# RWKV-7 stage of a fused three-block kernel: group norm a round later, hops over 0.86 of the round, 256-column scores, attention's first operands loaded in the last round

## The chip, the cores and the metric

The kernel runs on one core of a Trainium2 chip. The metric is the device time of one execution in microseconds, the median of several runs. The change is compared by the same median.

## The reference, cut to what matters

Three blocks follow one another on a residual stream of 1024 tokens by 1024 features, in float32: a mixing block (stick-breaking attention, HGRN and GLA), a block of RWKV-7 time mix plus dilated window attention, and a block of spatial gating plus Fourier mixing. The change touches the second one. Its RWKV part, for 16 heads of 64:

```python
xs = tuple(t.astype(jnp.float32).transpose(1, 0, 2, 3)
           for t in (r_h, w_h, k_h, v_h, -kk, kk * a_h))
def step(state, inp):
    r_t, w_t, k_t, v_t, av_t, bv_t = inp
    sa = jnp.einsum('bhvk,bhk->bhv', state, av_t)
    state = (state * w_t[:, :, None, :] + sa[..., None] * bv_t[:, :, None, :]
             + v_t[..., None] * k_t[:, :, None, :])
    return state, jnp.einsum('bhvk,bhk->bhv', state, r_t)
...
y = ((y - mu) * lax.rsqrt(var + GN_EPS)).reshape(B, S, RWKV_W) * ln_x_w + ln_x_b
bonus = jnp.sum(r_h * k_h * r_k, axis=-1, keepdims=True) * v_h
return (y + bonus.reshape(B, S, RWKV_W)) * jax.nn.silu(gate)
```

The scan is computed in chunks of 64 tokens. The window attention then works on q and k of the same block, in three dilations.

## The kernel before, in words

Every large projection is a float32 product made of three fp32r matmuls (operands split into a high and a low part; lines L310 to L312, called dense below). Weights come in on the SP queue (L280), ScalarE casts the high part (L281) and VectorE subtracts the low part (L282).

The RWKV stage (898 to 1932 us of the span) handles 16 units, each a pair of heads by half of the tokens (8 chunks of 64). It runs in 18 rounds `it`. In a round a planner, `interleave`, merges several generators: the one that is least far along its own stretch of the round goes next. A generator is given as (generator, number of steps n, a, b): its step k is due at a + (b - a) k / n of the round. `PLAN` holds a and b: [0] the chain, [1] the inverse, [2] the features, [3] the dense work. The compiled program fixes the order on every engine from this, engine by engine.

- `rw_feat`, unit `it`: decays, keys, bonus; then the scores, M1 and A, from 128x128 matmuls on tiles M and "At" (`BK`) into PSUM "mx" (L1116), masked by VectorE (L1118).
- `rw_inverse`, unit `it - 1`: a triangular inverse. A goes to DRAM (L1141) and back as "At" (L1143), 31 row steps run on VectorE (L1161 and L1163), the result goes by DRAM to XS (L1167, L1170), then small matmuls finish it (L1182, L1188). The features' `BK` and the inverse's At are one buffer.
- `rw_chain`, unit `it - 2`: the recurrence over 8 chunks in three hops each. h1 (L1219) reads the state SV, its result is copied to R by VectorE (L1220) and ScalarE (L1221). h2 (L1225) makes the corrected values in PSUM "ch", copied to SV by VectorE (L1226) and ScalarE (L1227). h3 (L1230) gives the next state (L1234 on VectorE, with sd of L1223), and L1235 the output. Behind the eighth chunk come two ScalarE evictions and the group norm: sums (L1242, L1248), a square root (L753 on VectorE, L754 on POOL), the scaling (L1250), four transposes into "ch" (L1257), four ScalarE evictions (L1261), and the bonus and the gate (L1263, L1264).
- `rw_dense` and `att_jobs`: projections; `ATT[it]` is how many attention projections a round takes.

Behind the 18 rounds the attention opens its pools, and `at_load` of its first unit U[0] fetches q and k (L1407, "qkr"), casts them (L1411, L1421) and subtracts (L1413, L1422); then the scores run (L1447).

Of the kernel before, what the change touches and what calls it, by code (L numbers as in the profile page):

```python
# [13 lines left out]
ALU = mybir.AluOpType  # L14
# [159 lines left out]
ATT = [1, 2] * 3 + [1, 0, 1, 1, 0, 1, 1, 1, 3, 2, 2, 2]  # L174
# [8 lines left out]
GNY = 8  # L183
# [6 lines left out]
QS = 1  # L190
RORD = [("gate", [128, 512], 2), ("tt", [128, 512], 2), ("sd", [128, 64], 2), ("R", [128, 64], 2), ("gst", [128, 24], 2),
        ("ast", [128, 512], 1), ("vst", [128, 256], 1), ("dc", [128, 8], 3), ("bv", [128, 512], 1), ("bw", [128, 512], 1),
# [8 lines left out]
PLAN = [(0.0, 1.0), (0.0, 0.5), (0.05, 0.8), (0.0, 1.0)]  # L201


class Kern:
# [774 lines left out]
    def rwkv(self):  # L979
        nc, tc, I = self.nc, self.tc, self.I  # L980
        with tc.tile_pool(name="rw", bufs=1, reuse_waits="tile") as rw, self.psum(mx=2, iv=1, ch=1, cy=1):
# [14 lines left out]
            att = iter(self.att_jobs())  # L996
            for it in range(18):
# [11 lines left out]
        self.rk_pool.__exit__(None, None, None)  # L1009
# [18 lines left out]
    def rw_feat(self, rw, S):
        nc, I = self.nc, self.I
        V, TT = nc.vector, nc.vector.tensor_tensor  # L1030
        ff = lambda n: self.t(rw, [128, 512], n, bufs=1)
# [7 lines left out]
        wa = self.t(rw, [128, 128], "wa", bufs=1)  # L1039
# [10 lines left out]
        e1 = self.t(rw, [128, 8, 65], "E1")  # L1050
# [18 lines left out]
        n2 = self.t(rw, [128, 8], "n2", bufs=2)  # L1069
# [18 lines left out]
        S["bv"] = self.t(self.dp, [128, 512], "bvd", bufs=3)  # L1088
        bv = self.t(rw, [128, 512], "bv", bufs=1)
# [5 lines left out]
        BK = self.t(rw, [128, 8, 128], "At", bufs=1)  # L1095
# [14 lines left out]
        for c0 in (0, 4):  # L1110
# [710 lines left out]
```

## Time and profile before

| what | value |
|---|---|
| median of 3 runs | 2780.82 us (2775.7 to 2782.38) |
| the profiled execution's own time | 2780.22 us |
| its span | 2778.4 us, mean granted clock 0.99 |
| TensorE busy over the span | 2693.8 us (97%) |
| VectorE | 1743.9 us (63%) |
| ScalarE | 1168.3 us (42%) |
| POOL | 262.0 us (9%) |
| DMA | 274.49 MB, mean 99 GB/s |

PE is TensorE's matmuls, PEld its weight loads, which overlap the matmuls; DVE is VectorE, ACT ScalarE, SP the engine whose queue issues most DMAs. A wait is put on the instruction that stood and on the one that released it. A busy share says little of a stage: the rows below are taken from the stages that the change touches.

### The profile page before, as it was taken

How to read it: one execution, taken by the hardware profiler on the slowest of the kernel's cores; microseconds unless marked ns; L12 is line 12 of the kernel's file. 1: busy time of each engine (PE TensorE's matmuls, PEld its weight loads, DVE VectorE, ACT ScalarE, POOL GpSimd, SP SyncE). 2: the span in 40 equal slices, each digit the busy share in tenths (PEclk: the TensorE clock that was granted, in tenths of full speed). 3: DMA queues.
4: the chain of work that ended last, by engine and by line, in shares of the span. 5: the costliest groups of instructions: out<-in, count | busy, mean ns of one | idle time of the engine just before them, and what ended most of it. 6: DMA issues, size and time to landing. Idle time of an engine off the chain costs nothing.

```text
span 2778.4 us, 49283 instructions
## 1 busy us (share of the span) xinstructions
PE 2693.8 (97%) x18584; PEld 2245.1 (81%) x18584; DVE 1743.9 (63%) x4636; ACT 1168.3 (42%) x2829; POOL 262.0 (9%) x366
## 2 busy tenths in 40 slices
PE   8999999999998999999999999999999999999999
PEld 7878787878776787778877777888889989978887
DVE  4675643443966568786788877673476776644344
ACT  4443323233323335444455455444565665432232
POOL 0000000000202000100111011000111211100100
PEclk9999999999999999999999999999999999999999
DMA  3111121115751322222222222223664553432132
GB/s 127 54 61 50 50 67 42 58 63 177 243 198 64 93 82 66 74 76 79 63 72 69 71 72 76 88 81 102 198 179 147 160 167 103 132 115 61 50 122 98
DMA packets 214142, 274.49 MB, mean 99 GB/s; under 512 B 70000, under 2 KB 105616, under 8 KB 213776
## 3 DMA queue, kind: packets, MB, share of 16 engines
q1 hardware_dynamic: 185904, 218.90, 26.4%
q10 hardware_dynamic: 28000, 52.44, 5.2%
q8 instruction: 146, 2.39, 0.4%
q14 instruction: 92, 0.75, 0.1%
HBM read 211.49 MB, written 59.77 MB: 98 GB/s over the span
## 4 chain that ended last, share of the span: by engine, by line
PE 42%; DVE 6%; issue 3%; ACT 3%; DMA 3%; POOL 1%; ACTq 0%; SPq 0%; DVEq 0%; POOLq 0%
PE pd L310 8%; PE pd L312 8%; PE pd L311 8%; PE po L1525 2%; PE mx L310 2%; PE mx L311 2%; PE mx L312 2%; PE mx L1116 1%; PE tr L1535 1%; PE sc L1447 1%; PE cy L1219 1%; PE sc L1448 1%; DVE wl L282 1%; DMA qkr<-qkg 1%; PE ch L1230 1%
## 5 line engine op out<-in xcount | busy, mean ns | idle before, releaser
L310 PE MATMUL pd<-aH,wh 128*128 128x512 f32 x1808 | 752.9, 417 | 11.9 <-ACT aH L305 7.9
L312 PE MATMUL pd<-aH,wl 128*128 128x512 f32 x1808 | 725.6, 401 | 2.2 <-DVE wl L282 2.2
L311 PE MATMUL pd<-aL,wh 128*128 128x512 f32 x1808 | 725.1, 401 | 1.4 <-DVE aL L306 1.4
L282 DVE TENSOR_TENSOR wl<-wraw,wh 128x512 fp32r<-128x512 f32 (+1 forms) x412 | 295.1, 722 | 287.1 <-ACT wh L281 282.7
L281 ACT CAST wh<-wraw 128x512 fp32r<-128x512 f32 (+1 forms) x412 | 249.8, 612 | 416.3 <-PE pd L311 221.9
L310 PEld LDWEIGHTS pd<-aH,wh 128*128 128x128 f32 x1808 | 344.8, 191 | 74.5 <-ACT aH L305 8.1
L312 PEld LDWEIGHTS pd<-aH,wl 128*128 128x128 f32 x1808 | 344.0, 190 | 72.8 <-DVE wl L282 3.6
L311 PEld LDWEIGHTS pd<-aL,wh 128*128 128x128 f32 x1808 | 345.1, 191 | 58.0 <-DVE aL L306 2.3
L310 PE MATMUL pd<-wh,aH 128*128 128x256 f32 (+1 forms) x976 | 288.1, 297 | 4.5 <-ACT wh L281 2.7
L311 PE MATMUL pd<-wl,aH 128*128 128x256 f32 (+1 forms) x976 | 279.2, 287 | 2.6 <-DVE wl L282 2.6
L312 PE MATMUL pd<-wh,aL 128*128 128x256 f32 (+1 forms) x976 | 277.1, 286 | 0.3 <-DVE aL L306 0.3
L310 PEld LDWEIGHTS pd<-wh,aH 128*128 128x128 f32 x976 | 186.0, 191 | 8.5 <-ACT wh L281 3.5
L311 PEld LDWEIGHTS pd<-wl,aH 128*128 128x128 f32 x976 | 186.5, 191 | 6.5 <-DVE wl L282 4.1
L312 PEld LDWEIGHTS pd<-wh,aL 128*128 128x128 f32 x976 | 186.1, 191 | 1.9 <-DVE aL L306 0.7
L1223 ACT ACTIVATE sd<-SV,dc 64x64 f32<-64x64 f32 x256 | 88.4, 345 | 106.3 <-DVE SV L1234 96.4
L1500 ACT ACTIVATE S<-S,anm 128x256 f32<-128x256 f32 (+1 forms) x256 | 118.1, 464 | 16.1 <-DVE anm L1493 16.1
L1161 DVE TENSOR_TENSOR Xt<-At,X 128x60 f32<-128x60 f32 (+24 forms) x496 | 105.1, 212 | 10.5 <-DMA At<-dA 1.0
L1163 DVE TENSOR_TENSOR X<-X,Xt 128x60 f32<-128x60 f32 (+24 forms) x496 | 105.2, 212 | 10.3
L1451 DVE CUSTOM_DVE_ANT_0 S<-sc,cf 128x256 f32<-128x256 f32 (+1 forms) x256 | 85.8, 377 | 38.9 <-PE sc L1448 25.7
L1219 PEld LDWEIGHTS cy<-SV,M 128*128 128x128 f32 x512 | 81.4, 189 | 23.8 <-DVE SV L1234 11.7
L1447 PE MATMUL sc<-kk,qq 128*128 128x256 f32 (+1 forms) x256 | 91.3, 371 | 7.8 <-DVE kk L1422 6.9
L1448 PE MATMUL sc<-kk,ql 128*128 128x256 f32 (+1 forms) x256 | 86.8, 350 | 0.0
(385 smaller groups left out, 4653.6 us busy)
## 6 DMA issues: line engine op xcount, KB each, us to landing
wraw<-in_w2fm SPq DMA_DIRECT2D x122, 256.0 KB, 2.8
wraw<-in_w1fm SPq DMA_DIRECT2D x80, 256.0 KB, 2.6
qkr<-qkg SPq DMA_DIRECT2D x152, 128.0 KB, 2.9
wraw<-in_w2out SPq DMA_DIRECT2D x64, 256.0 KB, 3.3
sgd<-s ACTq DMA_DIRECT2D x48, 256.0 KB, 2.2
sgt<-sgd SPq DMA_DIRECT2D x48, 256.0 KB, 3.5
qkg<-ast ACTq DMA_DIRECT2D x40, 256.0 KB, 2.1
wraw<-in_w3fm SPq DMA_DIRECT2D x38, 256.0 KB, 2.6
```

The source lines that it names most:

```text
L281: nc.scalar.copy(h, raw)
L282: nc.vector.tensor_tensor(l, raw, h.bitcast(F32), ALU.subtract)
L310: mm(ps, lh, rh, start=start, stop=False)
L311: mm(ps, lh, rl, start=False, stop=False)
L312: mm(ps, ll, rh, start=False, stop=stop)
L1161: eng.tensor_tensor(tmp[:, :M, :n], At[:, j:j + 1, j + 1:32].to_broadcast([128, M, n]), X[:, :M, j:j + 1].to_broadcast([128, M, n]), ALU.mult)
L1163: eng.tensor_tensor(X[:, :M, j + 1:32], X[:, :M, j + 1:32], tmp[:, :M, :n], ALU.add)
L1219: nc.tensor.matmul(xy[:, c, n], M1[:, c, n], sv[:, c, n], start=c % 4 == 0 and n == 0, stop=False, skip_group_check=True)
L1223: nc.scalar.activation(sd[s], sv[s, c, n], AF.Identity, scale=dc[s])
L1447: mm(o, q, k, start=i == 0, stop=False, skip_group_check=True)
L1448: mm(o, ql, k, start=False, stop=i == len(args) - 1, skip_group_check=True)
L1500: nc.scalar.activation(x, x, AF.Exp, bias=nm[:, n, h, t:t + 1], accum_out=l[:, n, h, t:t + 1])
```

## The change

The group norm leaves the end of `rw_chain` and becomes a generator of its own, `rw_fin`, for unit `it - 3`, so a round later; the last one runs alone after the rounds. The hops' plan goes from 38 steps in (0, 1.0), of which 24 are hops, to 24 steps in (0, 0.86). The scores take two head halves in one 256-column matmul, per pair of chunks; the masks follow. The inverse is planned over (0, 0.9) in place of (0, 0.5), with six steps between the X loads and their use, the features over (0.03, 0.92). `at_load` of U[0] moves into round 17, and its eight loads from the ACT queue to SP. The gate is computed in even rounds. `rf` is a new pool for the features and the inverse that is closed ahead of round 17. The attention projections are spread so that each round holds about 48 dense steps.

```diff
-ATT = [1, 2] * 3 + [1, 0, 1, 1, 0, 1, 1, 1, 3, 2, 2, 2]
+ATT = [1, 2] + [0, 2] * 6 + [2, 2, 2, 3]
...
-GNY = 8
...
-QS = 1
...
-PLAN = [(0.0, 1.0), (0.0, 0.5), (0.05, 0.8), (0.0, 1.0)]
+PLAN = [(0.0, 0.86), (0.0, 0.9), (0.03, 0.92), (0.0, 1.0)]
...
             for it in range(18):
                 gens = []
+                if it == 17:
+
+                    rf_pool.__exit__(None, None, None)
+                    self.rk_pool.__exit__(None, None, None)
+                    self.aqk_pool = tc.tile_pool(name="aqk", bufs=1, side="right", reuse_waits="tile")
+                    self.aqk = self.aqk_pool.__enter__()
+                    self.AU = [dict(p=u % 8, hf=u // 8) for u in range(16)]
+                    gens.append((self.at_load(self.aqk, self.AU[0]), 4, 0.2, 0.9))
                 if it >= 2:
-                    gens.append((self.rw_chain(rw, U[it - 2]), 30 + GNY, *PLAN[0]))
+                    gens.append((self.rw_chain(rw, U[it - 2]), 24, *PLAN[0]))
+                if it >= 3:
+                    gens.append((self.rw_fin(rw, U[it - 3]), 6, 0.1, 0.75))
                 if 1 <= it <= 16:
-                    gens.append((self.rw_inverse(rw, U[it - 1]), 37, *PLAN[1]))
+                    gens.append((self.rw_inverse(rw, rf, U[it - 1]), 42, *PLAN[1]))
                 if it < 16:
-                    gens.append((self.rw_feat(rw, U[it]), 22, *PLAN[2]))
+                    gens.append((self.rw_feat(rw, rf, U[it]), 23, *PLAN[2]))
                 jobs = list(islice(att, ATT[it]))
-                gens.append((chain(*jobs, self.rw_dense(rw, it)), 32 * (it < 14) + 16 * (it == 15) + 16 * len(jobs), *PLAN[3]))
+                n = 32 * (it < 14 and it % 2 == 0) + 16 * (it % 2 == 1 and it < 14) + 16 * (it % 2 == 0 and it >= 2)
+                gens.append((chain(*jobs, self.rw_dense(rw, it)), n + 16 * len(jobs), *PLAN[3]))
                 interleave(gens)
+            for _ in self.rw_fin(rw, U[15]):
+                pass
             self.late_jobs = list(att)
...
-        if odd and p < 8:
+        if not odd and p:
             g = [self.t(rw, [128, 512], "gate", bufs=2) for _ in range(2)]
-            self.gate[p] = g
-            yield from self.dense_gen(self.I["w2fm"][25 + p], self.tanh_gate_ev(rw, g, ("ast", 1)), self.acts)
-
-    def rw_feat(self, rw, S):
+            self.gate[p - 1] = g
+            yield from self.dense_gen(self.I["w2fm"][24 + p], self.tanh_gate_ev(rw, g, ("ast", 1)), self.acts)
...
         rm = self.c("rmask")
-        for c0 in (0, 4):
-            cs = slice(c0, c0 + 4)
+        for c0 in range(0, 8, 2):
+            cs = slice(c0, c0 + 2)
+            pv = self.mm_ps().rearrange("p (c n t) -> p c n t", c=2, n=2)
+            for c in range(2):
+                nc.tensor.matmul(pv[:, c].rearrange("p n t -> p (n t)"), BK[:, c0 + c], M1[:, c0 + c].rearrange("p n t -> p (n t)"),
+                                 start=True, stop=True)
             for n, (s, x, mk) in enumerate(((E, O, rm[:, 0:128]), (O, E, rm[:, 64:192]))):
-                ps = self.mm_ps()
-                pv = ps.rearrange("p (c t) -> p c t", c=4)
-                for c in range(4):
-                    nc.tensor.matmul(pv[:, c], BK[:, c0 + c], M1[:, c0 + c, n], start=True, stop=True)
                 for d, h in ((A, s), (M1[:, :, n], x)):
-                    TT(d[h, cs], pv[h], mk[h].unsqueeze(1).to_broadcast([64, 4, 128]), ALU.mult)
-                yield
+                    TT(d[h, cs], pv[h, :, n], mk[h].unsqueeze(1).to_broadcast([64, 2, 128]), ALU.mult)
+            yield
...
             nc.sync.dma_start(xs[o:o + 32, :, 64 * (g // 2) + b:64 * (g // 2) + b + 32], dX[g].rearrange("c r i -> r c i"))
-        yield
-
-        Y1 = self.t(rw, [128, 8, 32], "Xt", bufs=1)
...
             nc.tensor.matmul(xy[:, c].rearrange("p n v -> p (n v)"), A[:, c], both, start=False, stop=c % 4 == 3, skip_group_check=True)
             yield
-
-        y, sq, st = ff(), ff(), self.t(rw, [128, 24], "gst", bufs=2)
-        bc = lambda a: a.unsqueeze(2).to_broadcast([128, 8, 64])
+        S["y"] = y = self.t(rw, [128, 512], "tt", bufs=2)
         nc.scalar.copy(c8(y)[E], xy[E, :, 1])
         nc.scalar.copy(c8(y)[O], xy[O, :, 0])
+
+    def rw_fin(self, rw, S):
+
+        nc = self.nc
+        V, TT = nc.vector, nc.vector.tensor_tensor
+        p, hf, y = S["p"], S["hf"], S["y"]
+        E, O = slice(0, 64), slice(64, 128)
+        c8 = lambda a: a.rearrange("p (c t) -> p c t", c=8)
+        ff = lambda: self.t(rw, [128, 512], "tt", bufs=2)
+        gate = self.gate[p][hf]
+        bw = self.t(rw, [128, 512], "bw", bufs=1)
+        nc.sync.dma_start(bw, S["bv"])
+        sq, st = ff(), self.t(rw, [128, 24], "gst", bufs=2)
+        bc = lambda a: a.unsqueeze(2).to_broadcast([128, 8, 64])
         V.tensor_reduce(st[:, 0:8], c8(y), AX.X, ALU.add)
         V.tensor_scalar(st[:, 0:8], st[:, 0:8], -1.0 / 64, None, ALU.mult)
         TT(c8(y), c8(y), bc(st[:, 0:8]), ALU.add)
         nc.scalar.activation(sq, y, AF.Square)
         yield
-        yield
         V.tensor_reduce(st[:, 8:16], c8(sq), AX.X, ALU.add)
         self.rsqrt(rw, st[:, 16:24], st[:, 8:16], 1.0 / 64, 64e-5)
+        yield
+        yield
         TT(c8(y), c8(y), bc(st[:, 16:24]), ALU.mult)
-        for _ in range(GNY):
-            yield
+        yield
         z = ff()
         zv = z.rearrange("p (c two t) -> p c two t", two=2, t=64)
         yt = self.mm_ps("ch")
...
-                for _ in self.at_load(aqk, U[0]):
-                    pass
                 self.consts(at, "c3")
...
-                    (nc.scalar if p + hf == 0 and QS else nc.sync).dma_start(x[s], self.qkg[row][src, cols])
+                    nc.sync.dma_start(x[s], self.qkg[row][src, cols])
```

On TensorE, in the middle of a unit's hops before the change: h1 (L1219), the dense matmuls behind it, h2 (L1225) and h3 (L1230). `R` and `SV` are what the copies write.

```order
L1219 MATMUL cy_11414<-SV_1536_8924,M_1790_10421 128x64
L311 MATMUL pd_11561<-aL_1099_7105,wh_11452 128x512
L312 MATMUL pd_11561<-aH_1098_7104,wl_11453 128x512
L310 MATMUL pd_11561<-aH_1098_7104,wh_11452 128x512
L311 MATMUL pd_11561<-aL_1099_7105,wh_11452 128x512
L1225 MATMUL ch_11595<-R_11598,XS_1534_8922 128x64
L312 MATMUL pd_11561<-aH_1098_7104,wl_11453 128x512
L1068 MATMUL mx_11625<-cf_157,fs_11624 128x2 x4
L310 MATMUL pd_11561<-aH_1098_7104,wh_11452 128x512
L311 MATMUL pd_11561<-aL_1099_7105,wh_11452 128x512
L312 MATMUL pd_11561<-aH_1098_7104,wl_11453 128x512
L1230 MATMUL ch_11596<-SV_1536_8924,M_1816_10627 128x128
```

The changed program has new line numbers: dense is L308 to L310, h1 L1227, h2 L1233, h3 L1238, the transposes L1277. The same place in a unit's hops, on TensorE, in the changed program:

```order
L308 MATMUL pd_12201<-aH_1098_7104,wh_12084 128x512
L1227 MATMUL cy_11870<-SV_1536_8924,M_1881_10942 128x64
L1277 MATMUL ch_12217<-cf_157,tt_11846 128x128 x4
L1227 MATMUL cy_11870<-SV_1536_8924,M_1881_10942 128x64
L309 MATMUL pd_12201<-aL_1099_7105,wh_12084 128x512
L310 MATMUL pd_12201<-aH_1098_7104,wl_12085 128x512
L308 MATMUL pd_12201<-aH_1098_7104,wh_12084 128x512
...
L308 MATMUL pd_12201<-aH_1098_7104,wh_12090 128x512
L309 MATMUL pd_12201<-aL_1099_7105,wh_12090 128x512
L1233 MATMUL ch_12228<-R_12231,XS_1534_8922 128x64
```

The transposes, which stood behind the last hop, now stand between the two halves of an h1, and the next h2 takes the next tile of "ch". Between h1 and h2 there were four dense matmuls, now ten (five of them in the gap marked by dots).

On VectorE before the change, around the masks (L1118) of a unit; L1243 is of the norm, L1179 of the inverse:

```order
L947 SCALAR_TENSOR_TENSOR rkv_2564_14942<-last_14943,pf,rkv_2564_14942 128x1
L1243 TENSOR_SCALAR gst_15180<-gst_15180 128x8
L948 SCALAR_TENSOR_TENSOR rkv_2564_14942<-pd_15109,pf,rkv_2564_14942 128x511
L1118 TENSOR_TENSOR A_14991<-mx_15120,cf_8920 64x512
L1118 TENSOR_TENSOR M_2577_14989<-mx_15120,cf_8920 64x4x128
L1118 TENSOR_TENSOR A_14991<-mx_15140,cf_8920 64x512
L1118 TENSOR_TENSOR M_2577_14989<-mx_15140,cf_8920 64x4x128
L1118 TENSOR_TENSOR A_14991<-mx_15156,cf_8920 64x512
L1118 TENSOR_TENSOR M_2577_14989<-mx_15156,cf_8920 64x4x128
L1179 STREAM_TRANSPOSE Xt_15045<-XS_1534_8922 32x256
L1118 TENSOR_TENSOR A_14991<-mx_15171,cf_8920 64x512
L1118 TENSOR_TENSOR M_2577_14989<-mx_15171,cf_8920 64x4x128
```

On VectorE in the changed program, around the masks (L1129) of a unit; L1234 is the SV copy of a hop, L1242 the new state, L1228 the R copy:

```order
L1129 TENSOR_TENSOR A_15447<-mx_15534,cf_8919 64x256
L1129 TENSOR_TENSOR M_2661_15445<-mx_15534,cf_8919 64x2x128
L1129 TENSOR_TENSOR A_15447<-mx_15534,cf_8919 64x256
L1129 TENSOR_TENSOR M_2661_15445<-mx_15534,cf_8919 64x2x128
...
L1129 TENSOR_TENSOR M_2661_15445<-mx_15567,cf_8919 64x2x128
L1234 COPY SV_1535_8923<-ch_15551 64x64
L1129 TENSOR_TENSOR A_15447<-mx_15602,cf_8919 64x256
...
L1129 TENSOR_TENSOR M_2661_15445<-mx_15602,cf_8919 64x2x128
L1242 SCALAR_TENSOR_TENSOR SV_1535_8923<-ch_15552,dc_13916,sd_15553 64x64 x2
L1129 TENSOR_TENSOR A_15447<-mx_15624,cf_8919 64x256
...
L1129 TENSOR_TENSOR M_2661_15445<-mx_15624,cf_8919 64x2x128
L1228 COPY R_15640<-cy_15134 64x64
```

Where the masks were a block, hops' copies now stand among them, and each mask is half as wide.

On SP before the change, from the end of the RWKV stage into the attention; L227 is a constant, L1346 the residual r, L1407 are operands of attention:

```order
L280 DMA wraw_20201<-in_w2fm 128x512
L227 DMA cf_20069<-in_c 128x784
L1346 DMA r_3425_20030<-hd 128x1024
...
L1346 DMA r_3428_20033<-hd 128x1024
L1435 DMA ag_20155<-qkg 128x512
L1437 DMA vn_20156<-vd 128x4x128
L1346 DMA r_3421_20026<-hd 128x1024
L1346 DMA r_3422_20027<-hd 128x1024
L1407 DMA qkr_20071<-qkg 64x512 x2
L1407 DMA qkr_20111<-qkg 64x512 x2
```

On SP in the changed program, from the last weight loads of round 17 (L278) on; L1425 are the operands of U[0], L225 the constant, L1363 r:

```order
L278 DMA wraw_19756<-in_w2v 128x512
L1425 DMA qkr_19544<-qkg 64x512 x2
L1425 DMA qkr_19625<-qkg 64x512 x2
L1425 DMA qkr_19703<-qkg 64x512 x2
L1425 DMA qkr_19821<-qkg 64x512
L278 DMA wraw_19762<-in_w2v 128x512
L1425 DMA qkr_19821<-qkg 64x512
...
L278 DMA wraw_20348<-in_w2fm 128x512
L225 DMA cf_20072<-in_c 128x784
L1363 DMA r_3434_20062<-hd 128x1024
```

The loads of U[0] were on the ACT queue, and now stand on SP among weight loads, ahead of the constant and of r.

## Rows read from the trace of the kernel before

**Rows 1.** Windows, RWKV stage: length, busy (instructions) of PE, PEld, DVE, ACT, POOL, PEclk, DMA share, GB/s
```profile
898.00:1932.00 1034.00, 1007.56 (x6573) 822.28 (x6574) 756.61 (x2287) 476.16 (x1176) 96.39 (x151) 1.00 0.26 75
```
**Rows 2.** Waits of weight loads in the RWKV stage: us in total, times, longest
```profile
PEld ch L1230 <- ACT SV L1227: 25.4, 65, 1.1
PEld ch L1225 <- ACT R L1221: 24.3, 57, 1.5
PEld ch L1257 <- DVE tt L1250: 12.7, 7, 2.5
PEld cy L1219 <- DVE SV L1234: 11.7, 26, 1.1
```
**Rows 3.** Timeline at one h2 (start, us, engine line, [idle before and releaser])
```profile
1099.71 0.40 PE L312 MATMUL pd<-aH,wl 128*128 128x512 f32 x1
...
1099.94 0.40 PE L310 MATMUL pd<-aH,wh 128*128 128x512 f32 x1
...
1101.42 0.30 PEld L1225 LDWEIGHTS ch<-R,XS 128*128 128x128 f32 x2 [1.52 <-ACT R L1221]
```
**Rows 4.** Timeline at the transposes of one norm
```profile
1397.94 1.09 DVE L1250 TENSOR_TENSOR tt<-tt,gst 128x512 f32<-128x512 f32 x1 [1.83 <-POOL gst L754]
...
1399.09 0.66 PE L1257 MATMUL ch<-cf,tt 128*128 128x128 f32 x4 [1.94 <-DVE tt L1250]
```
**Rows 5.** Windows behind two long waits (columns as in rows 1)
```profile
1400.10:1403.50 3.40, 3.40 (x10) 2.62 (x9) 2.54 (x5) 3.27 (x8) 0.00 (x0) 0.50 0.00 0
1946.20:1953.00 6.80, 3.74 (x13) 3.35 (x14) 2.37 (x7) 1.83 (x3) 0.00 (x0) 0.50 0.87 275
```
**Rows 6.** Waits of weight loads from 1932 to 1965 us
```profile
PEld sc L1447 <- DVE kk L1422: 7.7, 2, 6.8
```
**Rows 7.** Timeline of the attention's start, SP, ACT and PE
```profile
1934.22 10.52 SPq L1346 DMA_DIRECT2D r<-hd  x4
...
1938.67 2.55 ACTq L1407 DMA_DIRECT2D qkr<-qkg  x4
...
1946.84 0.62 ACT L1411 CAST qq<-qkr 128x512 fp32r<-128x512 f32 x1 [4.97 <-DMA qkr<-qkg]
...
1949.26 0.48 PE L1447 MATMUL sc<-kk,qq 128*128 128x128 f32 x1 [6.41 <-DVE kk L1422]
```
**Rows 8.** Timeline, score matmuls (L1116), and 257-column ones (L1694), with the next dense
```profile
948.46 1.06 PE L1116 MATMUL mx<-M,At 128*128 128x128 f32 x8
949.27 0.47 PE L310 MATMUL pd<-aH,wh 128*128 128x512 f32 x1
...
2530.85 3.62 PE L1694 MATMUL mx<-dft,zc 128*128 128x257 f32 x16
2534.11 0.58 PE L310 MATMUL pd<-aH,wh 128*128 128x512 f32 x1
```
**Rows 9.** Groups of the RWKV stage by form: busy, mean ns, idle before
```profile
L1118 DVE TENSOR_TENSOR M<-mx,cf 64x512 f32<-64x512 f32 x64 | 44.1, 689 | 1.5
```
**Rows 10.** Groups of the whole span by form, a 128x256 VectorE instruction out of PSUM
```profile
L1330 DVE TENSOR_TENSOR r<-pd,r 128x256 f32<-128x256 f32 x64 | 26.6, 421 | 23.5 <-PE pd L312 23.0
```
**Rows 11.** Timeline at the transposes of another norm and the h2 behind
```profile
1614.28 0.66 PE L1257 MATMUL ch<-cf,tt 128*128 128x128 f32 x4 [1.50 <-DVE tt L1250]
...
1615.03 2.28 ACT L1261 ACTIVATE tt<-ch,pf 64x256 f32<-64x256 f32 x4 [0.45 <-PE ch L1257]
...
1617.37 0.43 PE L1225 MATMUL ch<-R,XS 128*128 128x64 f32 x2 [0.25 <-ACT tt L1261]
```
**Rows 12.** Timeline, SP's stores of A of two units
```profile
1017.94 3.03 SPq L1141 DMA_DIRECT2D dA<-A  x4
...
1075.40 0.80 SPq L1141 DMA_DIRECT2D dA<-A  x2
```
**Rows 13.** Timeline, VectorE's first and last row step of one unit
```profile
1031.60 0.18 DVE L1161 TENSOR_TENSOR Xt<-At,X 128x31 f32<-128x31 f32 x1
...
1063.77 0.18 DVE L1163 TENSOR_TENSOR X<-X,Xt 128x8 f32<-128x8 f32 x1
```

More of the change, by code (lines that the diff above doesn't have):

```diff
@@ L1017, in rw_dense, with rw_feat @@
         p, odd = divmod(it, 2)
-        if not odd and p < 7:
-            for n in (0, 1):
+        if p < 7:
+            for n in ((2,) if odd else (0, 1)):
                 yield from self.dense_gen(*self.rkv_args(p + 1, n))
-        if odd and p < 7:
-            yield from self.dense_gen(*self.rkv_args(p + 1, 2))
-        if odd and p < 8:
+        if not odd and p:
             g = [self.t(rw, [128, 512], "gate", bufs=2) for _ in range(2)]
-            self.gate[p] = g
-            yield from self.dense_gen(self.I["w2fm"][25 + p], self.tanh_gate_ev(rw, g, ("ast", 1)), self.acts)
-    def rw_feat(self, rw, S):
+            self.gate[p - 1] = g
+            yield from self.dense_gen(self.I["w2fm"][24 + p], self.tanh_gate_ev(rw, g, ("ast", 1)), self.acts)
+    def rw_feat(self, rw, rf, S):
         nc, I = self.nc, self.I
         V, TT = nc.vector, nc.vector.tensor_tensor
-        ff = lambda n: self.t(rw, [128, 512], n, bufs=1)
+        ff = lambda n: self.t(rf, [128, 512], n, bufs=1)
         p, hf, u = S["p"], S["hf"], S["u"]
@@ L1170, in rw_inverse @@
             nc.sync.dma_start(xs[o:o + 32, :, 64 * (g // 2) + b:64 * (g // 2) + b + 32], dX[g].rearrange("c r i -> r c i"))
-        yield
-        Y1 = self.t(rw, [128, 8, 32], "Xt", bufs=1)
-        Q = self.t(rw, [128, 8, 32], "X", bufs=1)
+        for _ in range(6):
+            yield
+        Y1 = self.t(rf, [128, 8, 32], "Xt", bufs=1)
+        Q = self.t(rf, [128, 8, 32], "X", bufs=1)
         qp = self.mm_ps("iv")
@@ L1201, in rw_chain @@
         svn = self.SV[(u + 1) % 2]
-        bw = self.t(rw, [128, 512], "bw", bufs=1)
-        nc.sync.dma_start(bw, bv)
-        gate = self.gate[p][hf]
-        ff = lambda: self.t(rw, [128, 512], "tt", bufs=2)
         c8 = lambda a: a.rearrange("p (c t) -> p c t", c=8)
@@ L1333, in proj @@
                     yield from self.tok_gen(I["w2out"][q][:, 8 * part:8 * part + 8], (H, L), range(lead, lead + 4 * len(hfs)), ev, lead)
-            with tc.tile_pool(name="at", bufs=1, reuse_waits="tile") as at, self.psum(**PB), \
-                    tc.tile_pool(name="aqk", bufs=1, side="right", reuse_waits="tile") as aqk:
-                U = [dict(p=u % 8, hf=u // 8) for u in range(16)]
+            with tc.tile_pool(name="at", bufs=1, reuse_waits="tile") as at, self.psum(**PB):
+                U, aqk = self.AU, self.aqk
                 self.at = self.jp = at
                 self.aeng = nc.vector if AB[4] else nc.gpsimd
-                for _ in self.at_load(aqk, U[0]):
-                    pass
                 self.consts(at, "c3")
@@ L1363, in attention @@
                     pass
+            self.aqk_pool.__exit__(None, None, None)
             self.open_acts("right")
```

27 lines of the change are left out of this document (15 added, 12 removed).

## The prediction, made before the changed kernel was run

> **What bounds the kernel now.** I read the busy times of the RWKV stage first (898 to 1932 us), then what TensorE's weight loads wait for there, then single waits in the timeline, then the granted clock behind the long ones, then the start of attention, and last the rows that price the parts. TensorE is busy for 1007.6 of the stage's 1034 us and VectorE for 756.6 [rows 1]. So TensorE's work sets the time, and a change can only take work off TensorE or take its waits away; moving work on the other engines is free as long as nothing new waits for it. The stage has two kinds of waits [rows 2]. Three belong to the chain's hops: h2 on its R copies (24.3 us), h3 on its SV copies (25.4) and the next h1 on the new state (11.7), 61.4 us in 148 waits. The fourth is the norm at the end of a unit: its transposes wait 12.7 us in 7 waits.
>
> How much of such a wait is lost? In the timeline two dense matmuls start 0.23 us apart (1099.71 and 1099.94), and the load of h2 shows a wait of 1.52 us and starts at 1101.42 [rows 3]. From start to start that is 1.48 us where 0.23 is the pace, so 1.25 us are lost, 0.27 less than the row says. I take 0.27 off every wait: the hops lose 61.4 - 148 x 0.27 = 21.4 us, the norm 12.7 - 7 x 0.27 = 10.8.
>
> **The norm a round later.** The wait is a serial tail: the last h3, the ACT evictions, sums on VectorE, a square root on POOL, the scaling L1250 (1.09 us from 1397.94, after 1.83 us of waiting for POOL), then the transposes, for which TensorE stands 1.94 us [rows 4]. In the changed order the sums and the scaling run among the next round's dense work, steps ahead of the transposes. Its bw load goes along, one SP issue a unit as before. The instructions are the same ones, so nothing is added, and I take the whole 10.8 us; the bounds are 10.8 and 0, the latter if the scaling is again the last thing before the transposes. The last unit's norm still runs alone behind its last h3; about 12 us of dense matmuls stand there in the order, so I count it as covered. If they do not cover it, it costs one wait like those of before, 2.5 us at most [rows 2].
>
> [...]
>
> **Attention's operands early.** The first scores of attention wait 7.7 us in 2 waits on VectorE's L1422 [rows 6], so 7.7 - 2 x 0.27 = 7.2 are lost. The chain reads back from 1949.26: ScalarE began its first cast at 1946.84 after 4.97 us of waiting for the q load, which was issued from the ACT queue at 1938.67, while SP's four 512 KB r loads, issued over 10.5 us from 1934.22, filled the same DMA engines [rows 7]. In the changed order the eight loads of U[0] stand on SP ahead of the constants and of the r loads, among weight loads of round 17, and the casts behind them have dense work beside them. On SP they are eight more issues, ahead of weight loads that are fetched some steps early; nobody waits. I take the 7.2 us. The clock is 0.50 again for 6.8 us behind this wait, with 3.74 us of work in them [rows 5]: 1.9 us. Both stand on one condition, that the loads land before TensorE gets there; with the loads as late as now they are worth 0.
>
> **The hops over 0.86 of the round.** Before, the 24 hops are steps of a generator with 38 steps, so they fill 24/38 = 0.63 of a round; now 0.86. I priced the matmuls that stand between a hop and the next one in either order. A gap is tight, for me, with under 1.0 us of work in it, since the longest waits for a copy are 1.1 to 1.5 us [rows 2]. Before, 158 of 384 gaps are tight, after it 79. Half of the tight gaps go, so I take half of the hops' loss: -10.7 us. The bounds are 0 (below, the first rival) and -21.4 (every one gone).
>
> **The transposes among the hops.** Now the four transposes take the PSUM buffer "ch" in the middle of the hops, and the h2 behind them needs the same buffer. At 1615.03 the four ACT evictions took 2.28 us and the h2 that waited for them began at 1617.37, 3.09 us after the transposes' start at 1614.28 [rows 11]. In the new order about ten dense matmuls, 2.3 us, stand between the transposes (0.66 us) and that h2, and ScalarE's R copy, some 0.2 us, is queued behind the evictions. That leaves 3.09 + 0.2 - 0.66 - 2.3 = 0.33 us, in 15 rounds: +5 us. Bounds: 0 when ScalarE is late elsewhere anyway, and 1.5 us a round (the 1.50 us by which the transposes themselves were held up there [rows 11], taken as what ScalarE may be late), 23 us.
>
> **The scores in 256 columns.** Eight records of 128 columns took 0.81 us up to the next dense matmul, 0.101 each; sixteen of 257 columns took 3.26, 0.204 each [rows 8]. Each f32 matmul makes two records, so 256 x 2 x 0.101 = 51.7 us become 128 x 2 x 0.204 = 52.2: 0. The masks become 256 of 64x256 in place of 128 of 64x512 at 0.689 us [rows 9]. The smaller form is not in the trace: half of 0.689 = 0.344 below, 0.421 for 128x256 out of PSUM above [rows 10]. VectorE gets 0 to 256 x 0.421 - 88.1 = 20 us more, of 277 us in which it is idle: nothing on the path.
>
> [...]
>
> **The rest** moves without adding. The inverse's row steps are spread by a plan of 0.9, six steps now lie between the X loads and their use, the gate is computed in even rounds, and each round has about 48 dense steps where there were 32 to 64. SP's queue keeps its number of issues apart from the eight.
>
> **The sum.** Against the profiled execution's own 2780.2 us (the median of the runs is 2780.8, so no correction): -10.8 - 1.7 (norm), -7.2 - 1.9 (attention), -10.7 (hops), +5.0 (transposes), 0 (scores) = 2752.9. I predict 2753 us.
>
> **Rivals.**
> *The hops keep their waits.* VectorE runs in order, and in the new order the hops' copies stand among runs of masks, where before the masks were a block with no hop inside. A copy behind one mask of 0.4 us is late by that much, which eats what the wider gaps give. For: each tight hop waits for a copy, not for arithmetic [rows 2]. Against: the masks are half as long each. Then the hop term is 0: 2763.6; at its worst the waits grow by as much as they would have shrunk, 2774.
>
> *The transposes hold the hops up* by the full 1.5 us a round: 2752.9 - 5 + 23 = 2771. For: TensorE did stand there once, even with no hop just behind [rows 11]. Against: ScalarE is busy for 476 of 1034 us [rows 1].
>
> *Slower: the rows of the inverse become the bound.* The features' BK and the inverse's At share one buffer, so one unit's loop is serial: from the dA stores at 1017.94 to the next ones at 1075.40 it took 57.5 us [rows 12], of which the rows took 32.4 (1031.60 to 1063.95) [rows 13]. I priced a middle round of the new order at 53.3 us of TensorE work plus about 1 of waits. If the loop cannot be done faster than this one was, each of 15 rounds grows to 57.5, 3.2 x 15 = 48 us: about 2801. It decides from a loop of 54.3 us on. For: the plan spreads the rows over 31/42 x 0.9 = 0.66 of a round, from 31/37 x 0.5 = 0.42. Against: in the built order VectorE has 73 to 107 instructions between a unit's first and last row, before it 78 to 110, so the rows are in fact as dense as they were, and no wait of rows 2 lies on a score or an inverse matmul.
>
> *The loads set the scores' pace.* Then half of 51.7 us goes: 2752.9 - 25.9 = 2727. Against: with one load a matmul, 257 columns took twice as long as 128 [rows 8].
> [...]
>
> **Chances.** Forecast 0.60 (its own range 2742 to 2764: hops from 0 to -21.4 with the transposes between), hops keep waits 0.15, transposes 0.12, inverse 0.08, loads 0.05. A difference of 0.3% (8.3 us, about what a measurement of this kernel can tell) puts faster below 2772.5 and slower above 2789.1. Faster: 0.60 + 0.05 and most of the next two, 0.18: 0.83. Same: their tails (2774 and both together, 2782): 0.09. Slower: 0.08. For 8 in 10 the range takes the forecast's low end with no clash (2737) and reaches to the transposes' case (2771): 2736 to 2772.
>
> **What would show it.** Right: the row of the transposes waiting for the scaling gone from the loads' waits; no wait over 1 us at attention's first scores and no 0.50 clock behind them; hop waits of about 30 us in 75 or so rows. The scores' records at 0.2 us. Wrong: h2 waiting for the eviction's tile (the transposes' clash); copies that show idle time behind masks; TensorE waiting at the scores or at the inverse's matmuls for VectorE, and rounds of over 54 us (the loop); a clock of 0.50 behind waits that were not there before.

## The result, and the profile of the changed kernel

The changed kernel takes 2755.45 us (median of 4 runs, 2750.08 to 2760.96), the kernel before beside it 2780.4 us: a ratio of 0.9916, interval 0.9901 to 0.9931. Forecast were 2753 us. In two later jobs, on two chips, the ratio was 0.9933 (0.9912 to 0.9953, the reference run f0 below) and, for a version whose only difference turned out to be a queue (e2), 0.9935. So the change is worth 18 to 25 us, where the forecast had 27.

The same stage, from its first feature matmul to the first score of attention: 1047.7 us before (901.53 to 1949.26), now 1032.9. Windows of the changed kernel, columns as in rows 1:

```profile
899.00:1931.90 1032.90, 1009.05 (x6363) 816.91 (x6363) 778.27 (x2424) 482.44 (x1189) 105.78 (x160) 1.00 0.27 79
```

That is 14.8 of the 22.4 us by which the spans differ (2778.4 and 2756.0). 5.1 lie behind the first score. The other 2.5 lie in front, in the first block, which the change does not touch. There the granted clock differs: the kernel before is at 0.50 for four stretches of 6.8 us, the changed one for three of 6.8 and three of 3.4. f0, the same kernel, reaches the stage at 890.2 us, 8.8 earlier than this profile, in an execution with a mean clock of 0.994 where this one has 0.991. So a single pair of traces is good to several microseconds only.

What the weight loads wait for between 898 and 1932 us, in the changed kernel (compare [rows 2]):

```profile
PEld ch L1233 <- ACT R L1229: 25.3, 53, 1.3
PEld ch L1238 <- ACT SV L1235: 18.7, 42, 1.6
PEld cy L1227 <- DVE SV L1242: 13.6, 21, 1.4
...
PEld iv L1194 <- DVE Xt L1191: 3.4, 3, 1.6
```

The row of the norm's transposes, which waited for the scaling, is gone. The three rows of the hops are not: 57.6 us in 116 waits, less 0.27 each 26.3 lost, where 21.4 were. And a row is new, the inverse's matmuls (L1194) on VectorE's transposes.

At attention's start the loads of U[0] are issued on SP from 1866.62 on, 62 us ahead of r, and the first score follows the dense matmul before it without a wait. Timeline of the changed kernel, SP and TensorE:

```profile
1866.62 12.06 SPq L1425 DMA_DIRECT2D qkr<-qkg  x7
...
1928.80 2.85 SPq L1363 DMA_DIRECT2D r<-hd  x4
...
1931.91 0.22 PE L1465 MATMUL sc<-kk,qq 128*128 128x128 f32 x1
```

The clash at "ch", timeline of the changed kernel behind one unit's transposes (1110.49):

```profile
1111.15 2.28 ACT L1281 ACTIVATE tt<-ch,pf 64x256 f32<-64x256 f32 x4 [0.40 <-PE ch L1277]
...
1113.02 0.39 PE L310 MATMUL pd<-aH,wl 128*128 128x512 f32 x1
...
1113.34 0.19 ACT L1229 COPY R<-cy 64x64 f32<-64x64 f32 x1
...
1113.59 0.43 PE L1233 MATMUL ch<-R,XS 128*128 128x64 f32 x2 [0.18 <-ACT R L1229]
```

The h2 starts at 1113.59; the dense matmul before it started at 1113.02, so 0.57 us passed in place of 0.23, 0.34 lost. This picture, an R copy behind the four evictions, occurs 9 times, with 0.32 to 0.34 us each.

The masks of 64x256 (VectorE, groups of the stage by form) take about as long as a 128x256 instruction [rows 10], not half of a 64x512 one:

```profile
L1129 DVE TENSOR_TENSOR M<-mx,cf 64x256 f32<-64x256 f32 x128 | 54.0, 422 | 2.3
L1129 DVE TENSOR_TENSOR A<-mx,cf 64x256 f32<-64x256 f32 x128 | 53.1, 415 | 5.8 <-PE mx L1125 5.0
```

### The profile page after: what moved, and what is told of

The parts are those of the page before. It is cut to its first block, busy times and chain, and to the rows that moved or that the text cites. A ratio compares the mean times of both kernels' runs of the same rounds, so it can differ in the third digit from the quotient of the medians.

```text
span 2756.0 us, 48859 instructions
## 1 busy us (share of the span) xinstructions
PE 2684.5 (97%) x18328; PEld 2232.9 (81%) x18328; DVE 1753.5 (64%) x4764; ACT 1167.4 (42%) x2829; POOL 265.1 (10%) x366
## 4 chain that ended last, share of the span: by engine, by line
PE 78%; DVE 10%; DMA 4%; ACT 3%; issue 3%; POOL 1%; SPq 0%; DVEq 0%; ACTq 0%; POOLq 0%
PE pd L308 17%; PE pd L310 16%; PE pd L309 16%; PE mx L308 2%; PE mx L309 2%; PE mx L310 2%; PE mx L1125 2%; PE po L1543 2%; PE tr L1553 2%; PE sc L1465 1%; PE cy L1227 1%; PE sc L1466 1%; PE mx L680 1%; DVE wl L280 1%; PE ch L1233 1%
## 5 line engine op out<-in xcount | busy, mean ns | idle before, releaser
L308 PE MATMUL pd<-aH,wh 128*128 128x512 f32 x1808 | 760.7, 421 | 12.0 <-ACT aH L303 7.9
L310 PE MATMUL pd<-aH,wl 128*128 128x512 f32 x1808 | 726.8, 402 | 3.4 <-DVE wl L280 3.4
L308 PEld LDWEIGHTS pd<-aH,wh 128*128 128x128 f32 x1808 | 344.7, 191 | 76.1 <-ACT aH L303 8.1
L310 PEld LDWEIGHTS pd<-aH,wl 128*128 128x128 f32 x1808 | 343.9, 190 | 75.1 <-DVE wl L280 5.5
L308 PE MATMUL pd<-wh,aH 128*128 128x256 f32 (+1 forms) x976 | 287.8, 296 | 5.0 <-ACT wh L279 4.3
L310 PE MATMUL pd<-wh,aL 128*128 128x256 f32 (+1 forms) x976 | 277.4, 286 | 0.1
L308 PEld LDWEIGHTS pd<-wh,aH 128*128 128x128 f32 x976 | 186.2, 191 | 8.6 <-ACT wh L279 5.4
L310 PEld LDWEIGHTS pd<-wh,aL 128*128 128x128 f32 x976 | 186.5, 192 | 1.9 <-DVE aL L304 0.6
L1227 PEld LDWEIGHTS cy<-SV,M 128*128 128x128 f32 x512 | 79.3, 190 | 24.7 <-DVE SV L1242 13.6
```

What stands on the lines that cost most here:

```text
L308: mm(ps, lh, rh, start=start, stop=False)
L310: mm(ps, ll, rh, start=False, stop=stop)
L1227: nc.tensor.matmul(xy[:, c, n], M1[:, c, n], sv[:, c, n], start=c % 4 == 0 and n == 0, stop=False, skip_group_check=True)
```

## The experiments

All times are medians of at least four runs; the ratio is to the kernel before, in the same job. e1 to e4 ran side by side, then f0, f2, e7 and e6, then e5, g4, f4 and g3; a letter and a number stand for each kernel.

Many of the differences below are no larger than what the clock makes alone: the mean granted clock of a run went from 0.988 to 0.996, and 0.002 of it is 5.5 us of 2755. An estimate takes this out: the span of each run times its mean granted clock, which counts a stretch at 0.50 as half lost. That is close to what the trace of the kernel before shows: dense matmuls start 0.43 us apart at 0.50 (1400.44 and 1400.87) and 0.23 at 1.00 [rows 3]. By it the kernel before came to 2749.1, 2751.9 and 2750.8 us in the three jobs of this section, so it repeats well. The table has the mean clock, and the difference to the kernel before of the same job, by the medians and at equal clock; the last column is good to 2 or 3 us. Whether a kernel itself raises or lowers the clock was not shown, so the medians still tell what it takes, and the last column what its waits are worth beside the clock.

| kernel | job | mean clock (kernel before) | by the medians, us | at equal clock, us |
|---|---|---|---|---|
| e2, the changed kernel but for a queue | 1 | 0.9924 (0.9916) | -18.2 | -15.9 |
| e1, hops over 0.63 | 1 | 0.9918 (0.9916) | -12.7 | -10.3 |
| e3, transposes in the other tag | 1 | 0.9946 (0.9916) | -28.1 | -18.1 |
| e4, norm back | 1 | 0.9939 (0.9916) | -0.4 | +6.0 |
| f0, the changed kernel | 2 | 0.9925 (0.9919) | -21.1 | -18.5 |
| f2, one pool | 2 | 0.9910 (0.9919) | -12.2 | -12.3 |
| e7, copies on ScalarE | 2 | 0.9937 (0.9919) | -27.2 | -21.1 |
| e6, inverse over 0.5 | 2 | 0.9936 (0.9919) | -16.3 | -10.9 |
| e5, scores in 128 columns | 3 | 0.9945 (0.9904) | -29.7 | -17.2 |
| g4, both spreads back | 3 | 0.9948 (0.9904) | -21.9 | -8.4 |
| f4, e3 and e7 together | 3 | 0.9928 (0.9904) | -28.9 | -20.3 |
| g3, f4 with hops over 0.95 | 3 | 0.9945 (0.9904) | -34.0 | -20.2 |

**f0, the changed kernel again.** 

> The changed kernel itself once more, as the reference for the three runs beside it on the same chip. Expected: 0.992 of the kernel before, no more than 0.002 from that.


Measured: 2756.03 us against 2777.13, 0.9933 (0.9912 to 0.9953).

**e4, the norm back in its own round** (with the hops' old pace, the gate in odd rounds and the old spread of the projections).
```diff
-gens.append((self.rw_chain(rw, U[it - 2]), 24, *PLAN[0]))
-gens.append((self.rw_fin(rw, U[it - 3]), 6, 0.1, 0.75))
+gens.append((chain(self.rw_chain(rw, U[it - 2]), self.rw_fin(rw, U[it - 2])), 38, 0.0, 1.0))
...
```


> The changed kernel with the norm back in its own round behind the hops, and with what belongs to that: 38 steps over the whole round (so the hops over 0.63), the gate in odd rounds, the old spread of the attention projections. Scores, inverse's plan and early operands stay as changed. Forecast: the norm's 12.5 us (10.8 of waits, 1.7 of clock) and the hops' 10.7 come back and the 5 of the transposes go, 18 us more than the changed kernel, about 2773.5 us. Rival (the hops' spread is worth nothing): the norm alone, less about 3 us of the transposes, 8 to 12 us more, 2763 to 2768 us. In both, the transposes wait for the scaling again, about 12 us in the wait rows.


Measured: 2773.76 us against 2774.14, 1.0000 (0.9991 to 1.0009). The waits of the transposes are back, in the loads' rows 8.7 us on the scaling and 4.4 more at the same place. TensorE's own rows, 905 to 1990 us:

```profile
PE ch L1273 <- DVE tt L1266: 9.6, 9, 1.6
PE mx L1132 <- DVE M L1125: 7.5, 7, 1.5
```

The second row, transposes of At into "mx" that wait for VectorE's masks, is new: in e1 and in the kernel before it is missing, and in the changed kernel it has 0.3 us. So e4 adds a wait of its own and is not the norm's undoing alone. It is 17.8 us above e2, the 18 that were expected, but not by the expected terms: its hop rows sum to 54.2 us in 155 waits, 12.3 lost, less than in the changed kernel. The number was met by luck.

**e1, the hops over 0.63 again.**
```diff
-PLAN = [(0.0, 0.86), (0.0, 0.9), (0.03, 0.92), (0.0, 1.0)]
+PLAN = [(0.0, 0.63), (0.0, 0.9), (0.03, 0.92), (0.0, 1.0)]
```


> The changed kernel with one number put back: the hops are planned over 0.63 of the round, as before, instead of 0.86. Theory of the forecast (the waits of the hops come from gaps with too little TensorE work, and wider gaps remove half of them): the hop waits come back, 10.7 us more than the changed kernel, about 2766 us, and wait rows of h2, h3 and h1 of about 60 us or more. Rival (a hop waits for copies that are queued behind other work of VectorE and ScalarE, which run in order, so wider gaps bring longer queues): no difference beyond 4 us, 2752 to 2759 us, with the waits' sum about the same in both.


Measured: 2761.47 us, 0.9962 (0.9949 to 0.9975). That is 5.5 us above e2 (below), whose rounds are the changed kernel's own, and 5.6 at equal clock: between the two theories in size, and not where the forecast had it: the hop rows sum to 61.3 us in 143 waits, 22.7 lost, less than in the changed kernel. What grew are the inverse's matmuls waiting for VectorE (9.2 us in 9 waits, 3.4 in 3 there) and a row of dense loads for which the profile shows no releaser (L308: 10.8 us in 14 waits, 3.9 in 12 there); the mean clock of the profiled execution is 0.991, where e2's is 0.993. e4, with the same pace of hops, is 12.3 us above e1 by the medians: the norm's place and the spread of the dense work together, with e4's new wait, so not the price of the norm alone.

**e6, the inverse over 0.5 again.**
```diff
-PLAN = [(0.0, 0.86), (0.0, 0.9), (0.03, 0.92), (0.0, 1.0)]
+PLAN = [(0.0, 0.86), (0.0, 0.5), (0.03, 0.92), (0.0, 1.0)]
```


> The changed kernel with the inverse planned over half of the round again (with its six steps behind the X loads kept). Forecast: the spread moves VectorE's work without adding any, 0, within 3 us of the changed kernel. Rival (rows in a block hold the copies of the hops up, and spreading them is what lets the hops through): waits of the hops up, 5 us or more above the changed kernel.


Measured: 2760.85 us, 0.9945 (0.9930 to 0.9959), 5 us above f0 by the medians, with overlapping intervals, and 7.6 at equal clock. Waits of the loads, 890 to 1990 us:

```profile
PEld ch L1233 <- ACT R L1229: 33.5, 61, 1.5
PEld ch L1238 <- ACT SV L1235: 26.7, 50, 3.0
PEld cy L1227 <- DVE SV L1242: 8.0, 19, 1.1
```

68.2 us in 130 waits, 33.1 lost, 7 more than in the changed kernel. The same sum is 25.9 to 27.5 in the traces of f0, e2 and f2, whose rounds are the changed kernel's, so the 7 are clear of what differs between executions: the rival had it right, rows in a block stand in the hops' way.

**g4, both spreads back.** `(0.0, 0.63), (0.0, 0.5)` in the same line.


> The changed kernel with both spreads put back together: hops over 0.63 and the inverse over 0.5 of the round. Each alone cost 5 to 6 us. Gap theory of the forecast (the hops' spread alone takes half of the hop waits): 11 us above the changed kernel, the same as with the hops alone put back or more. Queue theory (hops and rows share VectorE's queue; they get in each other's way when only one of them is spread): the two do not add up, 3 to 7 us above the changed kernel, and the hops' waits much like before the change, about 20 us lost.


Measured: 2758.49 us, 0.9921 (0.9906 to 0.9936): the changed kernel's own ratio, but at the highest mean clock of all, 0.9948. At equal clock g4 is 8.4 us below the kernel before, where the changed kernel is 15.9 to 18.5. Waits of the loads, 890 to 1990 us:

```profile
PEld ch L1238 <- ACT SV L1235: 24.3, 65, 1.6
PEld cy L1227 <- DVE SV L1242: 24.0, 35, 1.7
PEld ch L1233 <- ACT R L1229: 23.2, 66, 0.9
PEld pd L308 <- issue: 11.1, 16, 0.8
```

The hop rows sum to 71.5 us in 166 waits, 26.7 lost, as in the changed kernel; the row of dense loads is long again, as in e1. So at equal clock the two spreads together are worth some 7 to 10 us, and putting back either alone costs nearly as much (5.6 in e1, 7.6 in e6): only the pair pays. It does not show as fewer hop waits. g4 ran in another job than f0 and e2, so the 7 to 10 rest on the estimate.

**e7, all copies of a hop on ScalarE.**
```diff
-            V.tensor_copy(R[E], xy[E, c, 0])
+            nc.scalar.copy(R[E], xy[E, c, 0])
...
-            V.tensor_copy(sv[E, c, 0], up[E])
+            nc.scalar.copy(sv[E, c, 0], up[E])
```


> The changed kernel with all four copies of a hop on ScalarE; before, VectorE makes the first and ScalarE the second of each pair. Queue theory (a hop waits because its copies stand behind other work on two engines that run in order, first VectorE's queue, then ScalarE's): one of the two queues goes, and the waits of h2 and h3 (44 us in the loads' rows, some 17 to 18 lost) fall by a third to a half, 6 to 9 us less than the changed kernel. Gap theory of the forecast (the hop is short of TensorE work beside its copies, which take the same 0.2 us each on either engine): no difference beyond 3 us.


Measured: 2749.98 us, 0.9906 (0.9891 to 0.9922), 6 us below f0 by the medians, with intervals that just overlap, and 2.6 at equal clock, so the gain in time is not clear of the noise; the waits are. Waits of the loads, 890 to 1990 us:

```profile
PEld ch L1238 <- ACT SV L1235: 18.0, 49, 1.7
PEld cy L1227 <- DVE SV L1242: 17.7, 36, 1.0
PEld ch L1233 <- ACT R L1229: 16.9, 36, 0.7
```

The waits of h2 and h3 fall from 44.0 us in 95 (18.4 lost) to 34.9 in 85 (12.0 lost), by a third, as the queue theory said; h1's do not (8.0 lost, where 7.9 were). Here a wait that lies on a copy's queue was made shorter with the gaps left alone. The edit also takes away the hand-over from VectorE's copy to ScalarE's, which this run does not tell apart from VectorE's queue.

**e3, the transposes into the other PSUM tag.**
```diff
-        yt = self.mm_ps("ch")
+        yt = self.mm_ps()
```


> The changed kernel with the four transposes of the norm put into a buffer of PSUM tag mx instead of ch, so that the next h2 no longer needs the buffer that they hold. Forecast by its own term: 5 us less than the changed kernel, about 2750.5 us, and the waits of 0.33 us at the h2 behind the transposes gone. Rival (the h2 waits not for the buffer but for its R copy, which stands behind the four evictions on ScalarE whatever buffer they read): no difference beyond 3 us, and waits of about 0.3 us at that h2 stay, nine of them for 2.9 us in all.


Measured: 2746.05 us, 0.9905 (0.9889 to 0.9922), 0.0011 to 0.0030 below the changed kernel's ratios; at equal clock it is 2.2 us below e2, no more than the noise. Of the nine waits behind the evictions one is left (0.28 us), so 2.6 us are gone; the wait of 1.5 us at the inverse and its half clock are gone too (dense matmuls start 0.23 us apart there, from 1225 to 1252 us; another wait at the inverse, of 1.0 us, stays), since the order moved there as well. Whether the h2 had waited for the buffer or for the R copy alone is not told apart: the edit moved the transposes away from both.

**e2, attention's loads written later in the text.**
```diff
-                    gens.append((self.at_load(self.aqk, self.AU[0]), 4, 0.2, 0.9))
...
+                for _ in self.at_load(aqk, U[0]):
+                    pass
                 self.consts(at, "c3")
...
-                    nc.sync.dma_start(x[s], self.qkg[row][src, cols])
+                    (nc.scalar if p + hf == 0 else nc.sync).dma_start(x[s], self.qkg[row][src, cols])
```


> The changed kernel with the first operands of attention loaded where they were before: behind the rounds, ahead of the constant, from the ACT queue. Forecast: the wait of 7.2 us at the first scores and the half clock behind it (1.9) come back, 9.1 us more than the changed kernel, about 2764.5 us. Rival (the dense work that the changed order has left behind the last hop, or the load's new neighbours, hide it anyway): at most 2 us more, and no wait over 2 us at the first scores.


Measured: 2755.95 us, 0.9935 (0.9923 to 0.9948), and no wait at the first scores. It was no undoing: the loads are issued as early as in the changed kernel, from the ACT queue now; timeline of this kernel:

```profile
1865.20 0.49 ACTq L1426 DMA_DIRECT2D qkr<-qkg  x1
...
1870.17 0.62 ACT L1430 CAST qq<-qkr 128x512 fp32r<-128x512 f32 x1
```

So neither the place in the text nor the queue decides. f2 below looks at what is left, the tiles.

**f2, one pool again.**
```diff
-            rf_pool = tc.tile_pool(name="rf", bufs=1, reuse_waits="tile")
-            rf = rf_pool.__enter__()
+            rf = rw
...
```
The edit also opens the operands' pool behind the rounds, and writes its loads there, on the ACT queue.


> The changed kernel with the features and the inverse back in the pool of the whole stage (no pool of their own), the pool of attention's first operands opened behind the rounds and their loads on the ACT queue. In the run with the loads merely written later they were still issued 60 us ahead, so where they stand in the text does not decide; in this one the first load waits for a tile that POOL releases at the end of the stage, as before the change. Forecast: the wait at the first scores comes back, 7 us and some half clock behind it, 9 us more than the changed kernel. Rival (the dense work behind the last norm covers the late loads): at most 3 us more, and no wait over 2 us at the first scores.


Measured: 2764.92 us, 0.9965 (0.9951 to 0.9979), 8.9 us above f0 by the medians and 6.2 at equal clock. Waits of the loads from 1932 to 1965 us (compare [rows 6]):

```profile
PEld sc L1462 <- DVE kk L1437: 5.3, 2, 4.5
```

The half clock is back too, 0.51 from 1939.0 on for 6.8 us, and the first load is issued at 1928.2 us, 62 later than in the changed kernel. The forecast's 9.1 us are confirmed by the medians. As e2 rules out the queue and the place in the text, the cause is in the pools: the features' own pool is closed, and the operands' pool opened, ahead of round 17. f2 undoes both and does not tell them apart.

**e5, the scores in 128 columns again** (loop and masks as before the change).


> The changed kernel with the scores as before: 256 matmuls of 128 columns and 128 masks of 64x512. Forecast from the records of the kernel before (0.101 us for 128 columns, 0.204 for 257): TensorE's time for the scores is the same in both, so no difference beyond 3 us. [...] A smaller rival: the masks as four blocks of two put other gaps between the hops' copies, 3 to 6 us either way.


Measured: 2750.69 us, 0.9893 (0.9877 to 0.9909): not slower by the 25.9 us that the prediction's rival has for loads that set the scores' pace. By the medians it is about 5 us faster than the changed kernel, but at a clock of 0.9945 against f0's 0.9925; at equal clock it is 17.2 us below the kernel before, the changed kernel 15.9 to 18.5. So the 128 columns and the lighter masks together gain or cost nothing that can be measured. The hop rows are as they were (59.0 us in 119 waits, 26.9 lost). In its trace TensorE's longest wait at L1194 is 0.8 us, and the mean granted clock from 898 to 1900 us is 1.00.

**f4 and g3, towards a faster kernel.** f4 is e3 and e7 together, g3 has the hops over 0.95 besides.


> The changed kernel with the two edits that gained: the norm's transposes in the other PSUM tag, and all four copies of a hop on ScalarE. If the two act on different waits (the transposes on nine waits of 0.33 us and the order around the inverse, the copies on the queue of VectorE), they add up: 8 to 14 us below the changed kernel, 2742 to 2748 us. If both act through ScalarE's queue (the evictions stand ahead of the copies), the second gives nothing more: about 2749 us.

> The same two edits with the hops over 0.95 of the round instead of 0.86. Gap theory: wider gaps, 2 to 5 us less than without it. Queue theory: no difference beyond 3 us, or a little more, since the last hop of a unit comes closer to the first of the next.


Measured: f4 2751.5 us, 0.9899 (0.9879 to 0.9919), so the two edits do not add up; g3 2746.42 us, 0.9882 (0.9865 to 0.9899), the fastest of all. In g3 the hop rows are down to 34.7 us in 71 waits, 15.5 lost. Its interval lies below that of the changed kernel's first measurement and overlaps those of e3, e5, e7 and f4, so which of these is best is not settled; at equal clock e7, f4 and g3 are alike (-21.1, -20.3, -20.2). That g3 beats the kernel before by over 1% is settled.

## Why the prediction was right, step by step

The sum came out within 3 us of the first measurement. By the ratios of the two later jobs the changed kernel would have stood at about 2762 us in that first job, 9 above the forecast, so part of the nearness is luck: one step was wrong, and others were off in size.

**The norm** (-10.8 and -1.7): right in kind. Its row is gone, and in e4 the transposes wait again, 9.6 us on TensorE. A price for the norm alone was not measured. No run shows the 1.7 us of clock in the sum: the kernel before has 3.4 us at 0.50 behind the norm's wait [rows 5], and the changed kernel has 3.4 us at 0.50 as well, behind a wait at the inverse (below).

**Attention's operands** (-7.2 and -1.9): right, 8.9 us in f2. The forecast put the reason into the loads' place on SP and in the planner; e2 shows that this was not it. What makes them early is the pools.

**The hops** (-10.7): the step that failed is "half of the tight gaps go, so I take half of the hops' loss". The gaps widened, but the loss in the hops' rows did not fall: 21.4 us before, 26.3 after, 26.7 with both spreads put back. What the two spreads gain together, 7 to 10 us at equal clock by g4, does not come from fewer hop waits; beyond the longer row of dense loads in g4, where it comes from was not shown.

The step took the time from a hop's matmul to its consumer as fixed. It is not: a copy can stand behind work that the program has put ahead of it on its engine. Timeline of the changed kernel at its longest wait of h2 for an R copy:

```profile
1428.03 0.55 PE L1227 MATMUL cy<-SV,M 128*128 128x64 f32 x4
...
1428.46 0.75 DVE L1112 SCALAR_TENSOR_TENSOR M<-rkv,nkk,E 64x512 f32<-64x512 f32 x1
...
1429.47 0.69 DVE L1113 TENSOR_TENSOR M<-rkv,E 64x512 f32<-64x512 f32 x1
...
1430.63 0.22 DVE L1228 COPY R<-cy 64x64 f32<-64x64 f32 x1
...
1430.88 0.21 ACT L1229 COPY R<-cy 64x64 f32<-64x64 f32 x1 [2.28 <-DVE R L1228]
...
1431.14 0.30 PEld L1233 LDWEIGHTS ch<-R,XS 128*128 128x128 f32 x2 [1.29 <-ACT R L1229]
```

The copy of 0.22 us (L1228) begins 2.6 us after the h1 began: two feature instructions and row steps of the inverse went first. ScalarE, idle for 2.28 us, waits for VectorE's copy before it makes its own. Both engines keep the program's order in the traces: in the kernel before, VectorE's twelve instructions from L947 to the last of eight masks (L1118) start between 1493.29 and 1499.48 us in the order that the program has them in, and in the changed kernel ScalarE's R copy at 1113.34 us starts 1.56 us after VectorE's was done (1111.78), behind the four evictions that began at 1111.15.

The features were spread over more of the round as well, and so were the rows: where the hops went, VectorE's work went with them. The rival "the hops keep their waits" had the mechanism, though it named the masks: in e5, with its masks in fewer and longer pieces, the hops' waits are the same. e7, which takes one of the two queues away, cut the waits of h2 and h3 by a third, where the wider gaps had not.

The 0.27 us that the prediction takes off each wait are from one wait behind 512-column matmuls. At the wait shown here the matmuls ahead have 256 columns and start 0.12 us apart, and from the last of them (1429.77) to the h2 (1431.14) 1.37 us pass: of the 1.29 in the load's row all but 0.04 are lost. So the sums of what is lost are rough.

**The transposes** (+5.0): right in kind and in size of one, 0.33 us, but in 9 units rather than 15: about 3 us.

**The scores** (0): right, against the rival of the loads' pace, which e5 rules out: 256 loads more did not cost 26 us. Timeline of the changed kernel:

```profile
951.95 1.03 PE L1125 MATMUL mx<-M,At 128*128 128x256 f32 x4
952.63 0.58 PE L308 MATMUL pd<-aH,wh 128*128 128x512 f32 x1
953.04 0.40 PE L309 MATMUL pd<-aL,wh 128*128 128x512 f32 x1
```

Four records of 256 columns take 0.68 us up to the next dense matmul, less than the forecast's 0.2 each, but the one behind that matmul starts 0.41 us after it, where 0.23 is the pace. To the second dense matmul it is 1.09 us, where eight records of 128 columns took 1.13 before (948.46 to 949.59). The masks came out at the upper bound, 19 us more of VectorE (107.1 where 88.0 were), which the sum held to be free; e5, with the masks of before, is no faster at equal clock.

**The inverse's loop** as a bound: not the bound. The stores of A stand 52 to 65 us apart, which the forecast had named as its sign (over 54), but before the change they stood 51 to 71 apart; TensorE is busy for 1009.1 of the stage's 1032.9 us, and no row step waits for At's load.

**What the prediction left out**: a clock of 0.50 behind waits that were not there before was named as a sign against it, and there is one. Timeline and windows of the changed kernel:

```profile
1245.41 0.69 DVE L1271 TENSOR_TENSOR tt<-tt,gst 128x512 f32<-128x512 f32 x1 [1.83 <-POOL gst L752]
1246.13 0.43 DVE L1191 STREAM_TRANSPOSE Xt<-XS 32x256 f32<-32x256 f32 x1
...
1246.63 0.69 PE L1194 MATMUL iv<-Xt,A 32*32 32x32 f32 x30 [1.48 <-DVE Xt L1191]
...
1247.60:1251.00 3.40, 3.40 (x38) 2.04 (x36) 0.82 (x2) 2.20 (x7) 0.77 (x2) 0.50 0.02 5
```

The norm still has its wait for POOL's square root. It moved from TensorE's transposes to VectorE, where the scaling stands for 1.83 us and the inverse's transposes behind it, for which TensorE stands 1.48 us. So the terms are: -12.5 for the norm (10.8 by its row, and 1.7 of clock, an estimate: half of the 3.4 us at 0.50 in rows 5), -8.9 from f2, +3 for the transposes, about +4 for this wait and its clock, 0 for the hops: -14. Measured were 18 to 25 us; the 4 to 11 us between are not explained, as no term is known to better than some 4 us. In the pair of profiles 7.6 of the 22.4 us lie outside the stage, where these terms have little.

## What to carry to other kernels

Before pricing wider gaps between dependent steps, look at what the copies between them wait for: where they queue behind other work, as the copy here that began 2.6 us after its h1, room on the waiting engine need not shorten the wait, and taking the copy off that queue can: e7's waits of h2 and h3 fell from 44.0 us to 34.9. A wait that is moved a round later is gone only if nothing else stands behind it where it lands; look up who is queued behind the instruction that now waits. Before crediting an early load to where it is written, see when its tile comes free. Before believing a difference of a few microseconds between two kernels, compare the clocks at which they ran: here g4 and the changed kernel look alike by their medians and differ by 7 to 10 us at equal clock.

## What the runs showed of the hardware

The same wait in the same place left very different clocks behind it. In e2, whose stage differs from the changed kernel's only in the queue of a few loads, TensorE stood 1.52 us for L1191's counterpart, where it stood 1.48 us in the changed kernel; windows of e2:

```profile
1238.00:1251.60 13.60, 13.60 (x61) 7.94 (x61) 5.88 (x11) 8.09 (x20) 1.87 (x5) 0.50 0.17 54
```

13.6 us at 0.50 here, 13.7 in f2 behind a wait of 1.5 us, 3.4 in the profile of the changed kernel: with a stretch at 0.50 counted as half lost, an estimated difference of some 5 us between executions of nearly the same program. The kernels in whose traces TensorE stands there for at most 1.0 us also ran at a higher mean clock: e3 0.9946, e5 and g3 0.9945, e7 0.9937 and f4 0.9928, where e2, f0 and f2 had 0.9924, 0.9925 and 0.9910. But g4, with up to 1.3 us there, ran at 0.9948, and e6, with up to 1.9, at 0.9936. That the one causes the other was not tested.
